# ScalarE's small jobs parted around the exponentials in the neighbourhood attention of a hybrid encoder layer

## The chip, the cores and the metric

The kernel runs on one core of a Trainium2 chip. The time is that of the whole execution on the device in microseconds (us); lower is better. Of the core's engines the text speaks of PE (TensorE, matmuls; PEld are its weight loads), ACT (ScalarE), DVE (VectorE), POOL (GpSimd, which also issues loads) and SP (SyncE, which issues transfers, among them the transposes that the DMA engines do). Each engine works through its own list of instructions in order and waits at an instruction for the results of others.

## The reference

One layer over 1024 tokens of width 1024. One projection of the normalised input gives the columns of two head groups; group A attends to all tokens, group B to a neighbourhood on the token grid of 16 rows by 64 columns. Both are gated, joined, projected, added to the input and normalised.

```python
proj = rmsnorm(x, norm_gain) @ w_in                      # 1024 x 3328
q_a, k_a, v_a, g_a, q_b, k_b, v_b, g_b = split(proj)     # 512, 128, 128, 512, 4 x 512
q_a, k_a = rope(rmsnorm(q_a)), rope(rmsnorm(k_a))
o_a = softmax(q_a k_a^T / 8) v_a                         # 8 query heads, 2 key heads, all 1024 keys
o_b = softmax(q_b k_b^T / 8 + bias, in the window) v_b   # 8 heads, window 8 rows x 16 columns
mixed = concat(o_a * silu(g_a), o_b * silu(g_b))
out = rmsnorm(x + mixed @ w_out, final_norm_gain)
```

Everything is float32; the kernel works with pairs of half-precision numbers, a high and a low half, so that each product is three matmuls (high by high, high by low, low by high).

## The kernel before

Tokens are handled as 8 row blocks `u` of 128, weights as groups `g` of 256 columns: 0 to 12 for the input projection (11 and 12 are the gates of group B), 13 to 16 for the output projection. A group is loaded by POOL (`load_w`, L207), squared by ACT for its scale (`squares`, L357, four quarters, accumulating into `wss`), and split into halves (`split`): each quarter's high half on ACT (`hi`, L399), its low half on DVE (`lo`, L404). When the last quarter is split, the load of group `g + 2` is let go; for groups 15 and 16 the freed buffer takes two rows of the input for the residual (`have_x2`).

The stages follow each other: normalising and transposing x, the projections, group A's attention (64 slots, `a_qk`), and group B's attention. Group B's stage has 32 slots, one for each row block (in the order `ORDER` = 0, 7, 1, 2, ... 6) and pair of heads. In slot `i`, counted from 0:

- PE computes the scores of pair `i` (`b_scores`, L810 and L813, into one of three PSUM banks `sb` a head), then a filling of projection matmuls (L489) for the gates or the output, and the products with the values of pair `i - 3` (`b_pv`, L860 to L862);
- DVE makes the low half of pair `i - 1` (`b_lo`, L840), SP transposes both halves (L842), then DVE adds the bias to the scores of pair `i` and takes the maximum (`b_qk`, L831, two instructions, `nm`), which frees the banks; the results `t` go round three buffers;
- ACT takes two exponentials (L833) and the high halves of both (L835).

Around this small jobs are handed to ACT and DVE by the class `Flow`: `job(eng, cost, fn, delay, late, key)` puts a piece of work on a list, and `step` writes one slot: `pre`, ACT's jobs, `first` (here `b_lo` and `b_qk`), `mid`, DVE's jobs, `post`, the filling of PE, `last` (here `b_pv`). `work(eng)` takes jobs in order of `late` (0 is urgent) and age; those that are not urgent are taken only while the slot's budget lasts, which is `base[0] + 0.654 n - base[1]` for ACT and `- base[2]` for DVE, with `n` chunks of filling. So all of ACT's jobs of a slot stand ahead of its exponentials, and DVE's behind its bias additions. The jobs are:

- quarters: squares (0.75 or 1.0), `hi` and `lo`;
- gates (`g_gen`): ACT's tanh (L689), then DVE's product with the gate (L694), in the same slot; when a gate's product with the tanh is there, group B's heads are divided by their sums (L869 to L872) and multiplied in by POOL (L874);
- finished rows (`os_start`): the sum of squares of the mixed row, half of it on ACT (`sq`, L897) and half on DVE (`scale`, L901), POOL's root (L904), then in the next slot two casts on ACT (`hi`, L909) and their low halves on DVE (`lo`, L913), which SP transposes (L922). `ms[0]` is group A's half of the row, `ms[1]` group B's, and the squares' junk goes into the row's own buffer `mhl`, of which two take turns behind the fourth row;
- final norms (`fin_a`, L995, and `fin_b`).

POOL also issues the residual's loads (`load_x2`, L960).

## Time and profile before

| | us |
|---|---|
| runs shown | 568.47, 569.99, 571.41 |
| median | 569.99 |
| the profiled execution | 570.9, span 569.1 |
| stage of group B (32 slots) | about 366 to 516 |
| DVE busy in it | 59.75 of 74 to 440, 61.45 of 76 behind |

A row of the timeline is start, duration, engine, line, operation, result `<-` operands, shape and count, and in brackets the idle time just before with what ended it. A group's row ends in busy time, mean nanoseconds of one, and idle time before it. A row of waits is engine and line, for whom, total, times and longest. A row of stretches gives busy time and count of each engine, then the granted clock of PE as a share, the DMA engines' share and GB/s.

### The profile page before, as it was taken

Reading aid. Unit: us, or ns where it says so; the run is one execution under the profiler, and the core shown is the slowest. Engines: PE = TensorE matmul, PEld = TensorE weight load, DVE = VectorE, ACT = ScalarE, POOL = GpSimd, SP = SyncE. Lnnn points to the kernel's source line nnn. Section 1 sums busy time; section 2 is a strip of 40 time slices with the busy share of each in tenths; the row PEclk is TensorE's granted clock in tenths of the full one; section 3 lists DMA queues with packets and bytes.
Section 4 is the critical chain, followed back from the end, with each engine's and each line's share of the span. In section 5 each row is a group of like instructions: output and inputs, shape, how many; then the busy total and the mean of one; then the engine's idle time right before and its main releaser. Section 6 shows DMA issues by size and latency. Waiting matters only on the chain.

```text
span 569.1 us, 13780 instructions
## 1 busy us (share of the span) xinstructions
PE 516.9 (91%) x5583; PEld 403.1 (71%) x5583; DVE 444.3 (78%) x911; ACT 368.7 (65%) x583; POOL 154.2 (27%) x181
## 2 busy tenths in 40 slices
PE   2567989989999999999999999997999888999994
PEld 0455877768887555578888888886777566778883
DVE  3689688989977978788789897578788886987632
ACT  5546466958869669686786868285876686663211
POOL 2394887670000000000000034433621221213100
PEclk9978899999999999999999999999899798999998
DMA  8999739789999999998999989336576999998712
GB/s 242 214 182 225 128 61 212 126 144 182 228 229 185 172 213 196 197 186 162 237 162 200 187 185 184 97 75 155 125 128 114 192 199 204 164 149 156 202 38 74
DMA packets 244513, 95.47 MB, mean 168 GB/s; under 512 B 235489, under 2 KB 236001, under 8 KB 242530
## 3 DMA queue, kind: packets, MB, share of 16 engines
q1 hardware_dynamic: 240850, 73.89, 71.2%
q0 software_dynamic: 3312, 19.92, 12.6%
q10 hardware_dynamic: 288, 0.79, 0.5%
q8 instruction: 43, 0.70, 0.5%
q14 instruction: 20, 0.16, 0.1%
HBM read 29.56 MB, written 4.19 MB: 59 GB/s over the span
## 4 chain that ended last, share of the span: by engine, by line
PE 51%; DVE 11%; ACT 5%; issue 5%; DMA 5%; POOL 1%; SPq 0%; DVEq 0%; POOLq 0%; ACTq 0%
PE pj L489 19%; PE kb L489 7%; PE pjb L489 5%; DMA ar<-ar 4%; PE s L720 4%; PE s L722 4%; PE sb L489 3%; DVE ar L831 3%; PE pv L753 3%; PE pv L754 3%; PE pv L752 3%; ACT rq L833 2%; DVE ar L840 2%; DVE whl L404 1%; ACT ar L835 1%
## 5 line engine op out<-in xcount | busy, mean ns | idle before, releaser
L489 PEld LDWEIGHTS <-hT 128*128 128x128 f16 x2112 | 206.1, 100 | 61.3 <-DMA hT<-ar 17.3
L489 PE MATMUL pj<-whl,hT 128*128 128x256 f16 x1680 | 201.2, 278 | 22.4 <-DMA hT<-ar 10.4
L729 ACT ACTIVATE ar<-s,nm,sm 128x1024 f32<-128x1024 f32 x64 | 76.9, 1202 | 55.0 <-DVE nm L727 54.5
L727 DVE CUSTOM_DVE_ANT_0 ar<-s,sm 128x1024 bf16<-128x1024 f32 x64 | 82.0, 1281 | 32.4 <-PE s L722 32.1
L489 PEld LDWEIGHTS <-ar 128*128 128x128 f16 x768 | 74.6, 99 | 11.2 <-issue 2.2
L735 DVE TENSOR_TENSOR ar<-ar 128x1024 f16<-128x1024 f32 x64 | 79.5, 1242 | 1.4 <-ACT ar L730 1.4
L730 ACT ACTIVATE ar<-ar 128x1024 f16<-128x1024 f32 x64 | 67.6, 1057 | 2.1 <-DVE sum L759 0.3
L833 ACT ACTIVATE rq<-ar,nm 128x384 f32<-128x384 f32 (+1 forms) x64 | 34.1, 579 | 33.4 <-DVE nm L831 32.8
L489 PE MATMUL pjb<-whl,ar 128*128 128x256 f16 x408 | 48.9, 278 | 0.0
L489 PE MATMUL kb<-hT,whl 128*128 128x512 f16 x192 | 44.5, 379 | 0.0
L840 DVE SCALAR_TENSOR_TENSOR ar<-rq,ar 128x768 f16<-128x768 f32 (+1 forms) x32 | 30.8, 962 | 15.8 <-ACT ar L835 15.5
L753 PE MATMUL pv<-va,ar 128*128 128x64 f16 x384 | 40.0, 194 | 0.0
L752 PE MATMUL pv<-va,ar 128*128 128x65 f16 x384 | 39.9, 193 | 0.0
L754 PE MATMUL pv<-va,ar 128*128 128x65 f16 x384 | 39.8, 192 | 0.0
L752 PEld LDWEIGHTS <-ar 128*128 128x128 f16 x384 | 35.5, 96 | 5.3
L404 DVE SCALAR_TENSOR_TENSOR whl<-raw,sm,whl 128x512 f16<-128x512 f32 x52 | 39.1, 790 | 0.0
L753 PEld LDWEIGHTS <-ar 128*128 128x128 f16 x384 | 35.3, 97 | 5.3
L720 PE MATMUL s<-kTa,rq 128*128 128x512 f16 x128 | 38.0, 379 | 0.0
L207 POOL DMA_DIRECT2D raw<-in_w_dram x11 | 6.7, 608 | 111.3 <-ACT ar L730 89.0
L489 PE MATMUL pjb<-whl,hT 128*128 128x256 f16 x288 | 35.5, 281 | 0.0
L754 PEld LDWEIGHTS <-ar 128*128 128x128 f16 x384 | 35.4, 99 | 0.0
L874 POOL TENSOR_TENSOR ar<-ar,qkg 128x256 f32<-128x256 f32 x16 | 17.5, 1091 | 65.6 <-DVE qkg L872 64.4
(173 smaller groups left out, 972.7 us busy)
## 6 DMA issues: line engine op xcount, KB each, us to landing
raw<-in_w_dram POOLq DMA_DIRECT2D x11, 1024.0 KB, 7.4
raw<-in_wo_dram POOLq DMA_DIRECT2D x4, 1024.0 KB, 5.4
ar<-in_x_dram SPq DMA_DIRECT2D x7, 512.0 KB, 6.6
khh<-ar SPq DMA_DIRECT2D x16, 128.0 KB, 3.3
x2b<-in_x_dram POOLq DMA_DIRECT2D x4, 512.0 KB, 5.8
x<-in_x_dram POOLq DMA_DIRECT2D x4, 512.0 KB, 6.8
out_dram<-x2b SPq DMA_DIRECT2D x8, 256.0 KB, 3.6
out_dram<-x SPq DMA_DIRECT2D x7, 256.0 KB, 2.9
```

The costliest lines, as they stand in the source:

```text
L404: dve.scalar_tensor_tensor(wp[g][1][:, q], raw[g][:, q], col(S_ + g), wp[g][0][:, q], op0=OP.mult, op1=OP.subtract)
L489: pe.matmul(*o[0], **o[1])
L720: pe.matmul(s[:, c * 512:(c + 1) * 512], q, kTa[:, 4 * c:4 * c + 4, hh], start=True, stop=False)
L727: dve.tensor_tensor_reduce(out=hl[:, 1].bitcast(BF16), in0=s, in1=col(SHA).to_broadcast([P, 1024]), scale=col(NSA), scalar=3e38, op0=OP.ad ...
L729: act.activation(p32, s, AF.Exp, bias=nm, scale=col(SCA))
L730: at(0, "mid", lambda: act.activation(hl[:, 0], p32, AF.Copy))
L735: dve.tensor_tensor(hl[:, 1], p32, hl[:, 0], op=OP.subtract)
L752: pe.matmul(o, pt[:, kt], va[:, kt, hh, v_hi], start=kt == 0, stop=False)
L753: pe.matmul(o[:, :D], pt[:, kt], va[:, kt, hh, v_lo], start=False, stop=False)
L754: pe.matmul(o, pt[:, 8 + kt], va[:, kt, hh, v_hi], start=False, stop=kt == 7)
L833: act.activation(p32[:, e], t[:, e], AF.Exp, bias=nm, scale=-1.0)
L840: dve.scalar_tensor_tensor(hl[:, 1], p32, 2.0 ** 14, hl[:, 0], op0=OP.mult, op1=OP.subtract)
```

## The change

`step` now passes a limit, `early` = 1.2, to ACT's jobs ahead of `first`; after `first` (with its exponentials) ACT's list is taken up again with what is left of the budget. The limit is looked at before each job. It holds in group B's stage alone. In that stage DVE's budget is smaller by 0.5 and ACT's by 0.3, and a quarter's low half counts 1.0 instead of 0.72. The two squares of a finished row are exchanged between ACT and DVE, and their junk goes to spare strips of the tiles `rest` (for the first row DVE's still to its own buffer).

```diff
-BASE_A, BASE_B = (1.8, 2.6, 2.9), (1.7, 1.3, 1.5)
+BASE_A, BASE_B = (1.8, 2.6, 2.9), (1.7, 1.6, 2.0)
...
-    def work(self, eng):
+    def work(self, eng, early=None, more=False):
         b = self.budget.get(eng)
-        self.left[eng] = 1e9 if b is None else min(self.left.get(eng, 0.0), 0.5 * b) + b
+        if not more:
+            self.left[eng] = 1e9 if b is None else min(self.left.get(eng, 0.0), 0.5 * b) + b
+        stop = -1e9 if early is None else self.left[eng] - early
         while True:
             due = sorted(j for j in self.jobs if j[3] == eng and j[1] <= self.slot and (j[0] == 0 or j[4] / 2 < self.left[eng]))
-            if not due:
+            if not due or self.left[eng] <= stop:
                 return
...
-        self.work("act")
+        self.work("act", self.early)
         if first:
             first()
+        if self.early is not None:
+            self.work("act", more=True)
...
-            job("dve", 0.72, lo, i, delay=0, late=0.5 if g > 11 else 2, key=g)
+            job("dve", 1.0 if "b" in late else 0.72, lo, i, delay=0, late=0.5 if g > 11 else 2, key=g)
...
         def sq():
-            act.activation(osp[u][0][:, cs[1]].bitcast(BF16), ms[1], AF.Square, accum_out=t[:, 0:1])
+            act.activation(late["r"][0][:, 2048:2560].bitcast(BF16), ms[0], AF.Square, accum_out=t[:, 0:1])
             job("dve", 0.95, scale, delay=0, late=0, key=("os", u))

         def scale():
-            dve.tensor_tensor_reduce(out=osp[u][0][:, cs[0]].bitcast(BF16), in0=ms[0], in1=ms[0], scale=1.0, scalar=t[:, 0:1],
+            junk = late["r"][1][:, 2048:2560] if k else osp[u][0][:, cs[1]]
+            dve.tensor_tensor_reduce(out=junk.bitcast(BF16), in0=ms[1], in1=ms[1], scale=1.0, scalar=t[:, 0:1],
...
-    fl.base = BASE_B
+    fl.base, fl.early = BASE_B, 1.2
```

Lines of the changed kernel are 5 to 6 higher than those of the kernel before (L404 is L409 there, L694 is L699). PE's list keeps its order but for the sums of squares of groups 14 to 16 (L373, four matmuls of one column each), which move by one to three slots. Three places show what moves.

DVE in slots 5 to 7 (`nm7_4` to `nm1_0`; `rest` are the halves of group 13). Before:

```order
L694 SCALAR_TENSOR_TENSOR ar_78<-ar_78,pjb1_5197 128x2x256
L404 SCALAR_TENSOR_TENSOR rest1_5102<-raw13_5039,sm_97,rest0_5101 128x512 x4
L421 RECIPROCAL sm_97<-sm_97 128x1
L840 SCALAR_TENSOR_TENSOR ar_78<-rq_79,ar_78 128x512
L831 ISA ar_78,nm7_6_5507<-sb2_5113,rq_79,sm_97 128x256
```

Now:

```order
L699 SCALAR_TENSOR_TENSOR ar_78<-ar_78,pjb1_5197 128x2x256
L409 SCALAR_TENSOR_TENSOR rest1_5102<-raw13_5039,sm_97,rest0_5101 128x512
L845 SCALAR_TENSOR_TENSOR ar_78<-rq_79,ar_78 128x512
L836 ISA ar_78,nm7_6_5497<-sb2_5113,rq_79,sm_97 128x256
L836 ISA nm7_6_5497 128x1
L836 ISA ar_78,nm7_7_5500<-sb0_5111,rq_79,sm_97 128x256
L836 ISA nm7_7_5500 128x1
L874 RECIPROCAL sumb0_0_5504<-pvb0_5115 128x4
L875 TENSOR_TENSOR sumb0_0_5504<-sumb0_0_5504,sm_97 128x4
L877 TENSOR_TENSOR qkg_85<-pvb0_5115,sumb0_0_5504 128x256
L409 SCALAR_TENSOR_TENSOR rest1_5102<-raw13_5039,sm_97,rest0_5101 128x512
```

The four low halves stood in one slot and now stand one a slot; the other two follow in the next two slots.

ACT in slots 15 and 16 (`nm2_6` to `nm3_1`; `mhl`, `os`: the finished rows 7 and 1; `pjb0`: a gate's bank; `whl14`, `raw15`: weights). Before:

```order
L909 ACTIVATE mhl7_5891<-ar_78,os7_5890 128x512 x2
L689 ACTIVATE ar_78<-pjb0_5196,sm_97 128x512
L833 ACTIVATE rq_79<-ar_78,nm2_6_6016 128x384
L833 ACTIVATE rq_79<-ar_78,nm2_7_6019 128x384
L835 ACTIVATE ar_78<-rq_79 128x768
L897 ACTIVATE mhl1_6035,os1_6034<-ar_78 128x512
L399 ACTIVATE whl14_6036<-raw14_5372,sm_97 128x512 x4
L833 ACTIVATE rq_79<-ar_78,nm3_0_6090 128x384
```

Now:

```order
L362 ACTIVATE rest0_5101,wss15_0_5670<-raw15_5668 128x512
L362 ACTIVATE rest0_5101,wss15_1_5671<-raw15_5668 128x512
L362 ACTIVATE rest0_5101,wss15_2_5672<-raw15_5668 128x512
L915 ACTIVATE mhl7_5887<-ar_78,os7_5886 128x512 x2
L838 ACTIVATE rq_79<-ar_78,nm2_6_6008 128x384
L838 ACTIVATE rq_79<-ar_78,nm2_7_6011 128x384
L840 ACTIVATE ar_78<-rq_79 128x768
L694 ACTIVATE ar_78<-pjb0_5196,sm_97 128x512
L902 ACTIVATE rest0_5101,os1_6027<-ar_78 128x512
L404 ACTIVATE whl14_6029<-raw14_5427,sm_97 128x512 x2
L838 ACTIVATE rq_79<-ar_78,nm3_0_6081 128x384
```

The tanh of the gate moved behind the exponentials and the cast of slot 15, squares moved ahead of the row's casts, the row's square writes to `rest0`, and two of the four quarters moved behind the exponentials of slot 16. Slot 17 has the same form: its tanh stands behind its exponentials. DVE's product with the gate keeps its place directly behind the bias additions of slots 15 and 17.

POOL around the last weight load (`raw16`) and the first loads of the residual. Before:

```order
L207 DMA raw16_6147<-in_wo_dram 128x2048
L874 TENSOR_TENSOR ar_78<-ar_78,qkg_85 128x256
L960 DMA x2b_6277<-in_x_dram 128x1x1024
L874 TENSOR_TENSOR ar_78<-ar_78,qkg_85 128x256
L960 DMA x2b_6277<-in_x_dram 128x1x1024
```

Now:

```order
L879 TENSOR_TENSOR ar_78<-ar_78,qkg_85 128x256
L381 TENSOR_TENSOR sm_97<-wss15_0_5670,mh_83 128x1
L966 DMA x2b_6271<-in_x_dram 128x1x1024
L212 DMA raw16_6273<-in_wo_dram 128x2048
L879 TENSOR_TENSOR ar_78<-ar_78,qkg_85 128x256
L966 DMA x2b_6271<-in_x_dram 128x1x1024
```

The weight load moved behind the first `x2b`, which waits on POOL for the last projection from `hT`. The first load into group 15's freed buffer, likewise, moved behind one more product (L874).

## The prediction

> **What bounds the kernel now.** I read the page first, then sums over stretches, then the waits of PE, and last the timeline around each of them. The page's first line, and three stretches: the stage that the change touches up to its middle, the rest of it, and the output projections behind it.

> ```profile
> span 569.1 us, 13780 instructions
> ...
> core 0: us, PE busy (x) PEld busy (x) DVE busy (x) ACT busy (x) POOL busy (x), PEclk, DMA share, GB/s
> 366.00:440.00 74.00, 69.66 (x759) 55.73 (x760) 59.75 (x151) 52.62 (x103) 27.54 (x29) 0.98 0.59 118
> 440.00:516.00 76.00, 65.76 (x718) 50.91 (x717) 61.45 (x165) 51.21 (x94) 16.99 (x21) 0.93 1.02 179
> 516.00:561.50 45.50, 45.45 (x443) 40.61 (x440) 24.97 (x71) 9.77 (x25) 7.12 (x12) 1.00 0.45 120
> ```

> The 32 slots of the neighbourhood stage lie between 366 and 516. Behind 516 PE has no gap (45.45 of 45.50), so whatever PE gains before 516 arrives whole at the end. Before 366 no engine's order changes. What PE loses in the stage is idle time and half clock. The waits of PE from 366 to 516, four of the nine gaps in its timeline (in brackets the idle time and what ended it), and the three stretches at half clock:

> ```profile
> PE sb L810 <- DVE nm L831: 7.0, 5, 3.3
> PE pvb L860 <- DMA ar<-ar: 4.0, 2, 2.7
> PE pvb L860 <- DVE qkg L872: 3.4, 2, 2.3
> ...
> 396.71 0.19 PE L860 MATMUL pvb<-rq,ar 128*128 128x65 f16 x1 [2.28 <-DVE qkg L872]
> 422.92 0.19 PE L860 MATMUL pvb<-ar 128*128 128x65 f16 x1 [1.15 <-DVE qkg L872]
> 443.37 0.48 PE L810 MATMUL sb<-khh,qTb 128*128 128x384 f16 x1 [3.35 <-DVE nm L831]
> 468.28 0.32 PE L810 MATMUL sb<-khh,qTb 128*128 128x384 f16 x1 [1.45 <-DVE nm L831]
> 478.90 0.20 PE L860 MATMUL pvb<-rq,ar 128*128 128x65 f16 x1 [2.68 <-DMA ar<-ar]
> ...
> 398.00:401.40 3.40, 3.40 (x19) 2.44 (x17) 2.41 (x7) 2.65 (x6) 3.40 (x4) 0.51 1.10 309
> 442.40:449.20 6.80, 5.83 (x27) 3.69 (x27) 6.53 (x17) 3.62 (x7) 1.15 (x1) 0.50 1.04 227
> 480.00:483.40 3.40, 3.40 (x17) 2.26 (x16) 2.74 (x10) 3.37 (x6) 0.55 (x1) 0.50 0.83 228
> ```

> The idle time is 7.0 + 4.0 + 3.4 = 14.4 us: by the scores 0.91, 3.35, 0.39, 1.45 and 0.90, by transposes 2.68 and 1.30, by DVE's division 2.28 and 1.15. The gaps of 2.28, 3.35 and 2.68 us each have a half-clock stretch beginning during them or within 1.5 us of their end; the gaps up to 1.45 have none. So I price a gap above 2 us with its clock: half of the PE time at half clock, 1.7 + 2.9 + 1.7 = 6.3 us. At stake are 20.7 us in all.

> Without them PE needs (74 - 4.3 - 1.7) / 18 = 3.8 us a slot. DVE is close behind: 61.45 us over the last 14 slots are 4.4 us a slot. PE may be one slot ahead of DVE, since scores go round three banks, two a slot. A slot in which DVE (or ACT, for which DVE waits at L840) needs more than about 7.6 us therefore stops PE, and one of 4 us does not.

> **The change part by part.**

> *(a) Quarters spread, slots 4 to 13: -6.0 us.* The two gaps at 387.69 (0.91) and 396.71 (2.28) stand behind bunches of four low halves on DVE:

> ```profile
> 381.91 3.76 DVE L404 SCALAR_TENSOR_TENSOR whl<-raw,sm,whl 128x512 f16<-128x512 f32 x4
> ...
> 391.71 2.73 DVE L404 SCALAR_TENSOR_TENSOR rest<-raw,sm,rest 128x512 f16<-128x512 f32 x4
> ```

> With the new costs the first bunch is three and one, the second one a slot. The slot of the first gap is shorter by one low half (0.9) and the five small factor operations behind it (0.9), the slot of the second by three low halves (2.0), and 0.8 to 1.8 us earlier already. Both gaps should go, and with the second its half clock (1.7). What moved out lands in slots 7 to 10, where DVE itself waited for ACT or PE, so it costs nothing there; without that cover it would be 0.7 us a quarter. At 422.92 (1.15) the chain came through an ACT that ran three squares and two casts ahead of the exponentials; now the squares fill time in which the casts waited. 0.91 + 2.28 + 1.70 + 1.15 = 6.0; if the last gap and the clock stay, 3.2.

> *(b) Squares exchanged, slot 16: -6.3 us.* ACT's square of the gated row waited for a transpose of the row before, because its junk output went into the buffer being transposed:

> ```profile
> 436.73 0.63 ACT L897 ACTIVATE mhl<-ar 128x512 bf16<-128x512 f32 x1 [4.58 <-DMA ar<-mhl]
> ...
> 437.35 2.54 ACT L399 ACTIVATE whl<-raw,sm 128x512 f16<-128x512 f32 x4
> 439.80 1.11 ACT L833 ACTIVATE rq<-ar,nm 128x384 f32<-128x384 f32 x2
> ...
> ACT mhl L897 <- POOL ar L874: 5.5, 4, 1.6
> ```

> Behind it stood four quarters and then the exponentials, for which DVE and then PE waited (the 3.35 us gap). Now the junk goes to a spare strip, the row squared is group A's, finished long before, and only two quarters stay ahead. That takes 4.58 + 1.27 us out of ACT's path, more than the gap. With the 2.9 of clock: 6.3, and 3.35 if the clock is lost anyway. The other waits of ACT for POOL at this square (5.5 us in four) end too; DVE's square now needs POOL's product, but it stands a whole slot behind it, so I cost it at nothing. Uncovered it would be POOL's 1.1 us once a row.

> *(c) Jobs behind the exponentials, slots 15 and 17: +9.1 us.* The new limit of 1.2 us is spent by the two casts of a mixed row (2 x 0.72 in the table of costs). The tanh of a gate is then put behind the exponentials of the same slot, but DVE's product that needs it still stands directly behind that slot's bias additions. Today tanh comes first:

> ```profile
> 428.35 1.34 ACT L909 ACTIVATE mhl<-ar,os 128x512 f16<-128x512 f32 x2 [0.57 <-POOL os L904]
> 429.60 0.67 ACT L689 ACTIVATE ar<-pjb,sm 128x512 f32<-128x512 f32 x1
> 430.17 1.11 ACT L833 ACTIVATE rq<-ar,nm 128x384 f32<-128x384 f32 x2
> ...
> 430.29 0.69 DVE L694 SCALAR_TENSOR_TENSOR ar<-ar,pjb 128x512 f32<-128x512 f32 x1 [0.25 <-ACT ar L689]
> ...
> 431.72 1.88 DVE L913 SCALAR_TENSOR_TENSOR mhl<-ar,os,mhl 128x512 f16<-128x512 f32 x2
> ...
> 433.59 0.94 DVE L840 SCALAR_TENSOR_TENSOR ar<-rq,ar 128x768 f16<-128x768 f32 x1
> ...
> L357 ACT ACTIVATE rest<-raw 128x512 bf16<-128x512 f32 x16 | 10.0, 624 | 0.3
> L835 ACT ACTIVATE ar<-rq 128x768 f16<-128x768 f32 (+1 forms) x32 | 25.3, 790 | 1.0
> L840 DVE SCALAR_TENSOR_TENSOR ar<-rq,ar 128x768 f16<-128x768 f32 (+1 forms) x32 | 30.8, 962 | 15.8 <-ACT ar L835 15.5
> ```

> In slot 15 ACT will do, after the cast of slot 14, three squares (3 x 0.62, with their sums some 2.3 us), two casts (1.3), two exponentials (1.1), the cast (0.8) and tanh (0.6): 6.1 us. DVE in that time has L840 (0.9) and two bias additions (1.2), so it waits some 4 us, and behind it stand the product (0.7), the division of the finished heads (0.8), both L913 (1.9) and the next L840 (0.9). Slot 17 is alike: two quarters, a square, two casts, the exponentials, the cast and tanh are 6.0 us against some 3 of DVE's, a wait of about 3. From the additions of slot 15 to those of slot 18 DVE then needs about 22 us, where PE has work for four slots, 15, and comes with less than a microsecond in hand: I take two gaps of PE, 2.6 and 3.1 us. Both are above 2 us, so with half clock of 3.4 us each it is 5.7 + 3.4 = 9.1. Bounds: 3 if DVE's lead hides half of it and the clock holds, 12.5 if each behaves like the gap of 3.35 with 6.8 us at half clock.

> *(d) Slots 20 to 23: -1.8 us.* Group 15's four quarters (ACT 2.5, DVE 2.7 us) stood in one slot with a row's square; spread, they end the gaps of 0.39 and 1.45. Bound: 0.

> *(e) Transfers: -2.7 us.* The burst before 478.9, as POOL issues it and as its transfers land (last column: us to landing), beside an undisturbed transpose and one with a single load (rows of three short stretches):

> ```profile
> 441.39 0.62 POOL L207 DMA_DIRECT2D raw<-in_wo_dram  x1 [1.88 <-DVE sm L421]
> ...
> 449.76 0.58 POOL L960 DMA_DIRECT2D x2b<-in_x_dram  x1 [3.24 <-PE sb L489]
> ...
> x2b<-in_x_dram POOLq DMA_DIRECT2D x1, 512.0 KB, 6.7
> x<-in_x_dram POOLq DMA_DIRECT2D x1, 512.0 KB, 7.9
> ar<-mhl SPq DMA_TRANSPOSE x2, 7.6
> ar<-ar SPq DMA_TRANSPOSE x1, 10.4
> ...
> ar<-ar SPq DMA_TRANSPOSE x1, 3.6
> ...
> ar<-ar SPq DMA_TRANSPOSE x1, 6.3
> ...
> 478.88 0.62 DVE L831 CUSTOM_DVE_ANT_0 ar<-sb,ar,sm 128x384 f32<-128x384 f32 x1 [3.88 <-DMA ar<-ar]
> ```

> Alone a transpose lands after 3.6 us, with one load beside it after 6.3, with two loads and two row transposes after 10.4. Group 15 is finished two slots later, so the first residual load `x` leaves this burst: about 3 of the 3.88 us go. PE's share was 2.68 + 1.7 = 4.4; I take 2.7. Against it, the last weight load (1 MB) is issued two slots later too, behind the first `x2b` on POOL, so transposes of slots 18 to 20 meet both. They have two slots until they are needed, 8 us, against an estimated 7 to 9. Bounds 0 and -4.4.

> *(f) Nothing:* the gaps of 0.90 (506.66) and 1.30 (514.44, a transpose beside a load) are not touched, or are replaced where group 16's quarters now fall. No instruction is added; operation counts and sizes stay.

> Sum: -6.0 - 6.3 + 9.1 - 1.8 - 2.7 = -7.7 us against the profiled execution's own 570.9 (its span of 569.1 and 1.8 around it): **563.2 us**. The median of the runs, 569.99, lies 0.9 lower, inside their spread, so I leave it there.

> [...]

> **The rivals.**

> *Slower: a job behind the exponentials stops DVE wherever its other half is due in the same slot.* Besides the two tanh this holds for quarters in slots 4, 20 and 26 (the third or second quarter's low half needs an ACT instruction behind the cast). Price: 12.5 for the tanh, 3 x 1.3 for the quarters (an exponential and a cast less what DVE does meanwhile), and (d) and (e) come to nothing: -6.0 - 6.3 + 12.5 + 3.9 = +4.1, **575.0**. It decides once DVE's waits for ACT at L694 and L404 exceed about 14 us. For it: DVE already waits 15.5 us for ACT at L840. Against: PE's slot of lead. 12 in 100.

> *No change: transfers bound the second half.* From 440 to 516 the DMA engines are busy at a share of 1.02 and the bytes stay. If transposes then land when they land now, any lead reaching slot 18 is given back: **570**. Against: shares of 1.04 to 1.10 stand in shorter stretches above. 18 in 100.

> *All of it: DVE hides the tanh.* 14.4 + 6.3 gone: **550**. Against: DVE at 4.4 us a slot. 8 in 100.

> [...] 10 in 100.

> **How the numbers follow.** The forecast has 52 in 100, its own range 558 to 567. A measurement here tells about 0.5% from no change, so faster is below 567.1 and slower above 572.8. Faster: the forecast but for its edge, the case of 550 and most of the last, 0.65. Same: no change and those edges, 0.20. Slower: its rival and what no-change spills over, 0.15. The range takes in no change and reaches to 556, halfway to the case of 550, (c) small and (e) whole: 556 to 571.

> **What would show it.** (a) no gap of PE between 385 and 425 above 0.6 us and full clock there; (b) no wait of ACT's square; (c) DVE waiting 3 to 4 us for ACT ahead of the gate's product in two places about 13 us apart, each followed by a gap of PE at the scores; (e) no transpose above 9 us. I am wrong if the two tanh waits are absent, or larger than 5 us each, or if waits for transposes grow beyond today's 4.0 us of PE.

## The result, and the profile after

Over twenty runs of each kernel the change takes 568.58 us against 571.66 (medians), a ratio of 0.9946 with a 95% interval from 0.9921 to 0.9972: faster by 3.1 us, where 7.7 had been forecast. The execution that was profiled took 566.36 us (span 564.5), 4.5 less than the one profiled before; it lies 2.2 below its own median, the earlier one 0.8 below its own. So the two traces show a difference of 4.5 us, some 1.5 more than the medians. The ratios, here and below, leave out an execution that is over 1.5% longer than the fastest of its kernel, and two of the traces below are of such executions, that of sq_only (582.02 us) and that of vf_scalar (575.49 us), each the longest of its kernel's runs.

The same three stretches of the kernel after the change; the stage now ends 4.5 us earlier, so the bounds are shifted by that:

```profile
span 564.5 us, 13778 instructions
...
366.00:440.00 74.00, 69.22 (x740) 55.10 (x738) 62.05 (x154) 55.00 (x108) 28.34 (x28) 0.98 0.61 121
440.00:511.50 71.50, 63.89 (x743) 50.68 (x742) 60.39 (x162) 49.61 (x94) 18.46 (x23) 0.98 1.02 190
511.50:557.00 45.50, 45.41 (x442) 40.56 (x440) 25.43 (x71) 8.49 (x22) 6.92 (x10) 1.00 0.44 120
```

The part behind the stage is unchanged: 45.41 of 45.50 us busy. All of the gain was made in the 32 slots. What PE waited for there, five of its gaps, and the waits of DVE that changed most:

```profile
PE sb L815 <- DVE nm L836: 9.1, 6, 2.7
PE pvb L865 <- DVE qkg L877: 1.5, 2, 0.8
PE pvb L865 <- DMA ar<-ar: 1.4, 1, 1.4
...
391.77 0.27 PE L815 MATMUL sb<-khh,qTb 128*128 128x256 f16 x1 [0.97 <-DVE nm L836]
395.71 0.19 PE L865 MATMUL pvb<-rq,ar 128*128 128x65 f16 x1 [0.73 <-DVE qkg L877]
435.31 0.32 PE L815 MATMUL sb<-khh,qTb 128*128 128x384 f16 x1 [2.33 <-DVE nm L836]
447.71 0.32 PE L815 MATMUL sb<-khh,qTb 128*128 128x384 f16 x1 [2.74 <-DVE nm L836]
466.31 0.32 PE L815 MATMUL sb<-khh,qTb 128*128 128x384 f16 x1 [1.88 <-DVE nm L836]
...
DVE ar L845 <- ACT ar L840: 7.5, 11, 1.5
DVE ar L699 <- ACT ar L694: 6.6, 2, 3.6
...
DVE ar L836 <- DMA ar<-ar: 0.5, 1, 0.5
```

The waits for transposes fell from 4.0 us to 1.4 and those for the division from 3.4 to 1.5, but the waits at the scores rose from 7.0 to 9.1. Two of those are new, 2.33 and 2.74 us, 12.4 us apart. Ahead of each of the two, DVE stands still for a tanh:

```profile
430.50 0.69 DVE L699 SCALAR_TENSOR_TENSOR ar<-ar,pjb 128x512 f32<-128x512 f32 x1 [3.62 <-ACT ar L694]
...
442.91 0.69 DVE L699 SCALAR_TENSOR_TENSOR ar<-ar,pjb 128x512 f32<-128x512 f32 x1 [2.97 <-ACT ar L694]
```

These are the two waits that term (c) describes. Where the 4.5 us came from is best seen in the time from DVE's first running maximum of slot 0 to those of later slots, read from the timeline; executions reach slot 0 up to 12 us apart, and this leaves that out. All runs that are told of below stand in one table:

| kernel (label of the run) | slots 0 to 15 | 15 to 19 | 19 to 24 | 24 to the end |
|---|---|---|---|---|
| before | 62.36 | 22.64 | 27.36 | 90.21 |
| after | 58.70 | 24.95 | 23.87 | 90.01 |
| sq_only | 62.09 | 20.89 | 31.54 | 89.69 |
| no_limit | 60.29 | 18.19 | 29.15 | 89.19 |
| tanh_free | 58.08 | 18.20 | 28.63 | 90.04 |
| vf_scalar | 58.52 | 24.95 | 28.64 | 89.95 |
| after_loads | 58.72 | 24.95 | 24.64 | 93.08 |
| tf_loads | 58.06 | 18.20 | 30.98 | 93.56 |
| narrow_dve | 59.37 | 24.94 | 24.35 | 89.97 |
| tf_loads_nd | 59.12 | 18.20 | 28.30 | 93.59 |
| tf_sp | 58.07 | 18.20 | 26.64 | 88.43 |
| tf_sp_raw | 58.08 | 18.19 | 25.85 | 88.89 |
| after_sp_raw | 58.71 | 24.95 | 23.59 | 88.87 |
| before_sp_raw | 61.75 | 22.62 | 24.66 | 90.47 |
| sq_sp_raw | 61.72 | 19.84 | 24.58 | 90.25 |
| nl_sp_raw | 60.31 | 18.18 | 26.01 | 87.89 |
| tf_sp_raw_nd | 58.58 | 18.19 | 26.59 | 88.83 |

Before and after differ by -3.7, +2.3, -3.5 and -0.2 us, in all -5.0; slot 0 is reached 0.5 later. The forecast had -6.0 for (a), +2.8 for (b) and (c), -4.5 for (d) and (e), and 0.

### The profile page after: what moved, and what is told of

Its sections match the earlier page's. It is cut to its first block, busy times and chain, and to the rows that moved or that the text cites. A ratio compares the mean times of both kernels' runs of the same rounds, so it can differ in the third digit from the quotient of the medians.

```text
span 564.5 us, 13778 instructions
## 1 busy us (share of the span) xinstructions
PE 515.5 (91%) x5583; PEld 402.4 (71%) x5583; DVE 446.0 (79%) x911; ACT 367.8 (65%) x583; POOL 157.2 (28%) x181
## 4 chain that ended last, share of the span: by engine, by line
PE 51%; DVE 9%; ACT 8%; issue 5%; DMA 4%; SPq 0%; POOL 0%; DVEq 0%; POOLq 0%; ACTq 0%
PE pj L494 19%; PE kb L494 7%; PE pjb L494 5%; PE s L725 4%; PE s L727 4%; ACT rq L838 3%; PE sb L494 3%; PE pv L758 3%; DMA ar<-ar 3%; PE pv L759 3%; PE pv L757 3%; ACT ar L840 3%; DVE ar L836 2%; DVE ar L845 2%; DMA x2b<-in_x_dram 1%
## 5 line engine op out<-in xcount | busy, mean ns | idle before, releaser
L494 PEld LDWEIGHTS <-hT 128*128 128x128 f16 x2112 | 204.9, 100 | 58.8 <-issue 16.2
L494 PE MATMUL pj<-whl,hT 128*128 128x256 f16 x1680 | 201.6, 278 | 20.9 <-DMA hT<-ar 7.8
L494 PEld LDWEIGHTS <-ar 128*128 128x128 f16 x768 | 74.6, 99 | 11.7 <-issue 2.6
L494 PE MATMUL pjb<-whl,ar 128*128 128x256 f16 x408 | 47.4, 273 | 0.0
L494 PE MATMUL kb<-hT,whl 128*128 128x512 f16 x192 | 44.5, 379 | 0.0
L409 DVE SCALAR_TENSOR_TENSOR whl<-raw,sm,whl 128x512 f16<-128x512 f32 x52 | 38.7, 770 | 2.8 <-ACT whl L404 2.8
L845 DVE SCALAR_TENSOR_TENSOR ar<-rq,ar 128x768 f16<-128x768 f32 (+1 forms) x32 | 30.7, 959 | 7.9 <-ACT ar L840 7.5
L404 ACT ACTIVATE whl<-raw,sm 128x512 f16<-128x512 f32 x52 | 34.0, 709 | 1.4 <-POOL sm L381 1.4
## 6 DMA issues: line engine op xcount, KB each, us to landing
ar<-in_x_dram SPq DMA_DIRECT2D x7, 512.0 KB, 6.3
x2b<-in_x_dram POOLq DMA_DIRECT2D x4, 512.0 KB, 6.9
x<-in_x_dram POOLq DMA_DIRECT2D x4, 512.0 KB, 6.2
```

Source lines behind the costliest of these rows:

```text
L409: dve.scalar_tensor_tensor(wp[g][1][:, q], raw[g][:, q], col(S_ + g), wp[g][0][:, q], op0=OP.mult, op1=OP.subtract)
L494: pe.matmul(*o[0], **o[1])
L845: dve.scalar_tensor_tensor(hl[:, 1], p32, 2.0 ** 14, hl[:, 0], op0=OP.mult, op1=OP.subtract)
```

## The experiments

Times are ratios to the kernel before on the same chip, with their 95% interval. In the kernels that move the tanh, lines behind the edit are one higher than in the changed kernel.

### One part of the change at a time

**sq_only**: the kernel before with the squares exchanged, and nothing else of the change.

```diff
-            act.activation(osp[u][0][:, cs[1]].bitcast(BF16), ms[1], AF.Square, accum_out=t[:, 0:1])
+            act.activation(late["r"][0][:, 2048:2560].bitcast(BF16), ms[0], AF.Square, accum_out=t[:, 0:1])
...
+            junk = late["r"][1][:, 2048:2560] if k else osp[u][0][:, cs[1]]
...
```

> The kernel before with nothing but the exchange of the two squares and their new junk strips. My theory: ACT's 4.58 us wait for the row transpose goes, with it PE's gap of 3.35 us at the scores of slot 16 and its half clock (2.9 us): about -6.3 us, ratio 0.989, and no wait of a square for a transpose. Rival, transfers bound the second half: the lead is handed back at the transposes of slots 20 to 31; PE's waits for transposes grow from 4.0 us to over 7 and the ratio is 0.995 to 1.000.

Measured: 0.9959 (0.9915 to 1.0002). The gap of 3.35 us at slot 16 is replaced by two small ones, and a gap at a transpose appears three slots later:

```profile
449.88 0.32 PE L810 MATMUL sb<-khh,qTb 128*128 128x384 f16 x1 [0.64 <-DVE nm L831]
455.02 0.32 PE L810 MATMUL sb<-khh,qTb 128*128 128x384 f16 x1 [1.12 <-DVE nm L831]
468.13 0.23 PE L860 MATMUL pvb<-rq,ar 128*128 128x65 f16 x1 [5.14 <-DMA ar<-ar]
```

Slots 15 to 19 are 1.75 us shorter, slots 19 to 24 are 4.2 longer. The ratio lies in the rival's range, and in this trace its mechanism is seen: what the squares give is taken by transposes. The trace is of the longest of the seven runs, 9.5 us late already at slot 0, so it doesn't tell how much of this the others had.

**no_limit** and **tanh_free**: the changed kernel with the two waits for a tanh taken away in two ways. The first drops the limit; the second lets the tanh go ahead of its slot's other jobs and leaves it out of the limit.

```diff
 no_limit
-    fl.base, fl.early = BASE_B, 1.2
+    fl.base, fl.early = BASE_B, None
 tanh_free
-    job("act", 0.7, lambda: act.activation(th, pt, AF.Tanh, ...), late=0)
+    job("act", 0.7, lambda: act.activation(th, pt, AF.Tanh, ...), late=-1 if "b" in late else 0)
...
 in work():
             self.left[eng] -= j[4]
+            stop -= j[4] if j[0] < 0 else 0
```

> The changed kernel without the limit of 1.2 us: all of a slot's small jobs of ACT stand ahead of the exponentials again. My theory: DVE's two waits for a tanh (3.62 and 2.97 us) go, and with them PE's gaps of 2.33 and 2.74 us and the half clock between them (1.7 us): -6.8 us against the changed kernel, 0.983 of the one before. Rival, the limit earns elsewhere what it costs here: quarters and squares ahead of the exponentials make DVE wait longer for the casts of the exponentials, new gaps of PE in slots 10 to 22, and the ratio stays at 0.993 to 0.997.

> The changed kernel, but a tanh goes ahead of the other jobs of its slot and does not count against the limit, so it and up to two casts stand ahead of the exponentials; quarters and squares stay behind. My theory: as without the limit, the two waits and their gaps go, -6.8 us against the changed kernel: 0.983 of the one before. Rival, DVE's own work (4.4 us a slot) bounds slots 15 to 18: the waits go but PE waits for DVE in the same slots and at most 3 us are won: 0.989 to 0.995.

Measured: 0.9928 (0.9895 to 0.9960) and 0.9915 (0.9885 to 0.9945). Both take DVE's two waits and PE's two gaps away, and both shorten slots 15 to 19 by the same 6.8 us (24.95 to 18.2). That is the price of (c). But neither time falls by that, and both traces have one long gap at a transpose (6.20 and 5.36 us). Nine of tanh_free's ten runs lie from 561.46 to 568.22 us; the one that was profiled is the shortest. The trace of tanh_free, the gap and the transfers from 438 to 462:

```profile
455.13 0.24 PE L866 MATMUL pvb<-ar 128*128 128x65 f16 x1 [5.36 <-DMA ar<-ar]
...
q1 hardware_dynamic: 7987, 2.00, 65.5%
q0 software_dynamic: 576, 2.62, 46.0%
...
x2b<-in_x_dram POOLq DMA_DIRECT2D x4, 512.0 KB, 8.5
raw<-in_wo_dram POOLq DMA_DIRECT2D x1, 1024.0 KB, 7.6
ar<-ar SPq DMA_TRANSPOSE x4, 13.9
```

Transposes that land after 3.7 us alone take 13.9 here, beside three residual rows and the last weight group. In the changed kernel the same loads stand at the same places, and the transposes landed within 8.3 us. Its row for 447 to 471:

```profile
q0 software_dynamic: 720, 3.15, 49.8%
...
ar<-ar SPq DMA_TRANSPOSE x6, 7.2
```

It isn't that the tanh only hid a wait of the same length. Counted from the issue of the first residual row, the weight load goes out after 2.37 us in both kernels, the next transpose after 3.10 and the second row after 6.29; that transpose landed after 7.6 us in one kernel and 13.9 in the other, and PE asked for it here 8.6 us after its issue. Of the four traces without the waits for a tanh and with these loads on POOL, all have a gap of 5.4 to 7.3 us at this place (no_limit, tanh_free, tf_loads, tf_loads_nd); of the four with these waits (after, after_loads, narrow_dve, vf_scalar) one has long transposes there, vf_scalar with 12.9 and 15.6 us, and its gaps are 2.67 and 1.10. What makes a transpose long in one execution and not in the other was not found.

**vf_scalar**: what kept the gaps of 0.97 and 0.73 us at 391 and 395? In slot 6 of the changed kernel a product of two columns took fifteen times its length (2.40 us against 0.16 in the trace before), until two additions on POOL had ended:

```profile
388.11 2.40 DVE L487 TENSOR_TENSOR vf<-sm 128x1 f32<-128x1 f32 x1
...
388.53 1.96 POOL L786 TENSOR_TENSOR ar<-ar,rest 128x384 f32<-128x384 f32 x2
```

```diff
-        dve.tensor_tensor(t, col(RC + VB + hh), col(G2 + GB - GATE + hh), op=OP.mult)
+        dve.tensor_scalar(t, col(RC + VB + hh), col(G2 + GB - GATE + hh), None, op0=OP.mult)
```

> The changed kernel with one instruction of another form: the 128x1 product of two columns, which took 2.40 us in the changed kernel's trace and 0.16 us in the one before, is a multiplication by a per-partition scalar, so that it reads one tensor. My theory: with two tensors from SBUF it was held up by the two POOL products that ran from 388.53 to 390.49; in the new form it takes under 0.3 us, PE's gap of 0.97 us at the scores behind it and that of 0.73 behind the next slot's division go: -1.7 us against the changed kernel, ratio 0.991 to 0.992. Rival, it waited for something else (its operand): it still takes over 2 us and the ratio is 0.994 to 0.996. Second rival: it is short now, but the next instruction of DVE takes the time.

Measured: 0.9944 (0.9914 to 0.9975). The second rival holds: the product is short, and the next instruction takes the time, again until POOL's pair ends (393.17 + 1.96 = 395.13):

```profile
392.75 0.21 DVE L487 TENSOR_SCALAR vf<-sm 128x1 f32<-128x1 f32 x1
393.00 2.16 DVE L488 TENSOR_SCALAR sm<-vf 128x4 f32<-128x4 f32 x1
...
393.17 1.96 POOL L786 TENSOR_TENSOR ar<-ar,rest 128x384 f32<-128x384 f32 x2
```

In no_limit a third instruction meets the pair (390.03 to 391.99), the addition at L845: it starts at 389.64 and takes 2.90 us, where the one of the slot before takes 0.68. So it is not this one form. Three different instructions, one of them with a single tensor as its operand, started 0.42, 0.17 and 0.39 us ahead of the pair and ended 0.02, 0.03 and 0.55 us behind its end. That is all the rows show; what holds the instruction up was not shown.

### The transfers: how many bytes, or beside what

**after_loads**, **tf_loads**: 2.5 MB of loads are held back, in the changed kernel and in tanh_free. The third residual row thus goes out in slot 21 in place of 20, the fourth in slot 25 in place of 21. In tf_loads the edits of tanh_free come on top.

```diff
-X2_BEHIND = {0: (0, 1), 1: (2,), 2: (3,), 3: (4,), 4: (5,), 5: (6,), 6: (7,)}
+X2_BEHIND = {0: (0, 1), 3: (2,), 4: (3,), 5: (4, 5), 6: (6, 7)}
...
-        if i == 25:
+        if i == 29:
             late["gout"] = one.tile([P, 1024], F32, tag="gain", name="gain_o")
```

> The changed kernel with 2.5 MB of loads held back: the third and fourth residual row come behind the row transposes of the fourth and fifth mixed row, the rows of the output's second half behind the sixth and seventh, the gain of the output norm four slots later; nothing else. My theory now: two waits lie one behind the other in slots 15 to 20, first DVE's for the two tanh, then PE's for transposes that meet the loads (4.9 us in the run with the tanh moved); the changed kernel pays only the first, so taking load away wins at most its gap of 1.42 at the transpose near 510: ratio 0.992 to 0.995. Rival, the transfers cost the changed kernel as much in most executions, only not in the one profiled: 0.985 to 0.989.

> The tanh ahead of its slot and outside the limit, and the 2.5 MB of loads held back. My theory: with both waits gone the gap of 5.36 us at slot 20 goes (transposes of slots 18 to 20 land within 9 us in place of 13.9 and 15.3), and the ratio is 0.980 to 0.984. Rival, transposes alone fill the DMA engines (about 0.74 of their time from 440 to 516): they still land after 10 us or more and the ratio stays at 0.989 to 0.993.

Measured: 0.9983 (0.9948 to 1.0017) and 0.9968 (0.9944 to 0.9993): worse than without the edit, outside what either theory gave. The gaps at transposes of tf_loads:

```profile
459.37 0.24 PE L866 MATMUL pvb<-ar 128*128 128x65 f16 x1 [7.29 <-DMA ar<-ar]
...
511.54 0.20 PE L866 MATMUL pvb<-rq,ar 128*128 128x65 f16 x1 [3.30 <-DMA ar<-ar]
```

The first is longer with 0.5 MB less beside it, the second (3.08 in after_loads) stands where the loads were moved to. My theory that the amount of data makes the wait falls. The trace's packet records tell more: in tf_loads the small packets of a transpose last 18 ns when it runs alone. From 455 to 459 us the mean is 117, because 220 of 563 packets last 50 to 708 ns, while 4 KB packets of a residual row from POOL's queue trickle in between (180 KB); the engines move 45 to 104 GB/s through most of it, against some 290 a little later, when transposes run alone. But a load of POOL's queue beside a transpose is not enough: in the changed kernel's trace 893 KB of such loads were moved from 455 to 459, and none of the 1537 transpose packets beside them lasted over 26 ns. So the question for the next runs is whether the long packets go when the loads leave POOL's queue.

**tf_sp**, **tf_sp_raw**, **after_sp_raw**: so the loads go through SP's queue, in line with the transposes, with the same issue points: in tanh_free the residual rows, then the last weight group too, then both in the changed kernel.

```diff
-            pool.dma_start(x2[u], rows_of(x, u, 1024, 0, 1024))
+            sp.dma_start(x2[u], rows_of(x, u, 1024, 0, 1024))
 and in tf_sp_raw and after_sp_raw
-        pool.dma_start(raw[g], w[g] if g < 13 else wo[g - 13])
+        (pool if g < 16 else sp).dma_start(raw[g], w[g] if g < 13 else wo[g - 13])
```

> The tanh ahead and outside the limit; the residual rows are loaded through SP's queue, in line with the transposes, in place of POOL's (the last weight group stays with POOL). My theory: a transpose is held up because a load from the other queue is moved at the same time (its packets took 18 ns alone and 50 to 150 ns beside such a load); in one queue they follow one another, transposes of slots 18 to 20 land within 10 us in place of 14 to 16, PE's gap of 5.4 to 7.3 us at slot 20 shrinks below 2, ratio 0.980 to 0.985. Rival, the bytes alone make it: the transposes wait behind the loads instead, the gap stays at 3 us or more and the ratio at 0.989 to 0.994.

> As the last, with the last weight group's 1 MB through SP's queue too. My theory: no load is left in the other queue in slots 18 to 21, transposes land within 10 us and the gap is below 2 us: 0.979 to 0.984. Rival: the transpose behind the weight group waits for its 1 MB as well, a gap of 3 us or more: 0.989 to 0.994.

> The changed kernel, the tanh where the change put them, with residual rows and the last weight group through SP's queue. My theory: the two waits for a tanh still take their 6 us, so that transposes have slack; only the gap of 1.42 us near 510 and the chance of a longer one go: 0.990 to 0.995. Rival, transfers cost the changed kernel most of what the forecast missed: 0.984 to 0.989.

Measured: 0.9817 (0.9781 to 0.9854), 0.9810 (0.9773 to 0.9848) and 0.9921 (0.9890 to 0.9953). All three ratios are as this theory had them. In the trace of tf_sp, which keeps one load on POOL's queue, the slowest transpose still took 10.5 us and the gap 2.09, just over what the theory allowed. The five runs of tf_sp_raw lie between 558.35 and 560.81 us, closer together than those of tanh_free. Its trace over the same 24 us, and the gaps above 1 us:

```profile
453.33 0.20 PE L866 MATMUL pvb<-ar 128*128 128x65 f16 x1 [1.10 <-DMA ar<-ar]
460.31 0.33 PE L816 MATMUL sb<-khh,qTb 128*128 128x384 f16 x1 [2.19 <-DVE nm L837]
...
q1 hardware_dynamic: 10724, 5.16, 100.7%
...
x2b<-in_x_dram SPq DMA_DIRECT2D x4, 512.0 KB, 7.5
raw<-in_wo_dram SPq DMA_DIRECT2D x1, 1024.0 KB, 6.7
ar<-ar SPq DMA_TRANSPOSE x5, 7.8
```

5.16 MB went through this queue where tanh_free moved 4.62 through both, and transposes landed after 7.8 us in place of 13.9. In the six traces with all these loads in SP's queue no transpose from slot 15 on took over 9.5 us. The loads changed three things at once, the queue, the engine that issues them and the kind of queue that the page names (`hardware_dynamic` for `software_dynamic`); which of them counts was not separated. With the tanh left where the change put them (after_sp_raw) 6 to 7 us are missing again: 24.95 against 18.19 in slots 15 to 19.

### The terms again, with the transposes out of the way

**before_sp_raw** (the kernel before, loads in SP's queue), **sq_sp_raw** (the same with the squares exchanged), **nl_sp_raw** (no_limit with loads in SP's queue): edits as above.

> The kernel before with nothing but residual rows and the last weight group loaded through SP's queue. My theory: only its waits for transposes go (gaps of 2.68 and 1.30 us and the half clock behind the first, 1.7 us): 0.990 to 0.994; the gap of 3.35 at slot 16 stays, since no load is near it. Rival: loads in line with transposes delay those as much as they delayed them from the side, 0.997 to 1.002.

> The same with the squares exchanged too. My theory: the term forecast for the squares (3.35 us of gap and 2.9 us of half clock) now arrives whole: 0.011 below the run with the loads alone, that is 0.979 to 0.984. Rival, the lead is taken back further on by DVE, as the transposes took it when the squares were exchanged alone: at most 0.005 below.

> The changed kernel without the limit of 1.2 us, loads in SP's queue. My theory: the limit wins nothing that the costs and the exchange don't, so this equals the run with the tanh ahead of the limit and the loads in SP's queue, 0.979 to 0.984. Rival: squares and quarters ahead of the exponentials cost 2 us or more in slots 10 to 22, 0.985 to 0.990.

Measured: 0.9941 (0.9915 to 0.9967), 0.9898 (0.9862 to 0.9935), 0.9805 (0.9767 to 0.9843). The first is as expected, at the upper edge. The exchange of the squares brings 0.0043, not 0.011; here the rival's bound holds, though the two intervals overlap. In the traces, the gap at slot 16 of before_sp_raw and then those of sq_sp_raw in its place:

```profile
440.90 0.32 PE L810 MATMUL sb<-khh,qTb 128*128 128x384 f16 x1 [3.33 <-DVE nm L831]
```

```profile
441.47 0.32 PE L810 MATMUL sb<-khh,qTb 128*128 128x384 f16 x1 [0.62 <-DVE nm L831]
446.61 0.32 PE L810 MATMUL sb<-khh,qTb 128*128 128x384 f16 x1 [1.12 <-DVE nm L831]
```

Slots 15 to 19 go from 22.62 to 19.84: the term is worth 2.8 us. The limit, whose effect nl_sp_raw shows against tf_sp_raw, can't be told from nothing in the ratios (0.9805 and 0.9810); in the single traces slots 0 to 15 are 2.2 us shorter with it and slots 24 to the end 1.0 longer. Against the kernel before both are faster by 11 us, against the changed one by some 8.

**narrow_dve**, **tf_loads_nd**, **tf_sp_raw_nd**: the eight additions of POOL's, of which a pair holds up DVE in slot 6, are given to DVE itself, in the changed kernel, in tf_loads and in tf_sp_raw.

```diff
-        pool.tensor_tensor(bias[hh][:, h4i], bias[hh][:, h4i], late["inner"], op=OP.add)
+        dve.tensor_tensor(bias[hh][:, h4i], bias[hh][:, h4i], late["inner"], op=OP.add)
```

> The changed kernel with the eight additions 128x384 that POOL makes in slots 6 to 9 made by DVE at the same places. My theory: the 2.2 us by which an instruction of DVE is held in slot 6 until POOL's pair ends are gone, against two additions of some 0.5 us on DVE; the gap of 0.97 us at slot 6 and that of 0.73 at slot 7 go: the stage is shorter by 1 to 1.7 us, ratio 0.991 to 0.993. Rival, DVE's own 4 us more take back what the collision cost: 0.994 to 0.997, and gaps in slots 7 to 9.

> All three: tanh ahead and outside the limit, loads held back, the additions on DVE. My theory: the terms add, 0.978 to 0.982. Rival: with DVE as the bound the last of them wins nothing, 0.983 or more.

> The tanh ahead, all these loads in SP's queue, and the eight additions of slots 6 to 9 on DVE in place of POOL. My theory: 1 to 1.7 us less than with the additions on POOL, 0.978 to 0.979. Rival: DVE's own work takes it back in slots 7 to 12, 0.981 to 0.983.

Measured: 0.9932 (0.9897 to 0.9968), 0.9994 (0.9957 to 1.0031), 0.9842 (0.9800 to 0.9884). Gaps of narrow_dve up to the first tanh:

```profile
390.96 0.19 PE L865 MATMUL pvb<-rq,ar 128*128 128x65 f16 x1 [0.44 <-DVE qkg L877]
399.76 0.19 PE L865 MATMUL pvb<-ar 128*128 128x65 f16 x1 [0.61 <-DVE qkg L877]
408.21 0.19 PE L865 MATMUL pvb<-rq,ar 128*128 128x65 f16 x1 [0.92 <-DVE qkg L877]
417.20 0.19 PE L865 MATMUL pvb<-ar 128*128 128x65 f16 x1 [0.99 <-DVE qkg L877]
432.65 0.32 PE L815 MATMUL sb<-khh,qTb 128*128 128x384 f16 x1 [2.32 <-DVE nm L836]
```

This execution reaches slot 0 3.3 us before that of the changed kernel. The product of 2.40 us takes 0.16 here, the gap of 0.97 has gone and that of 0.73 is 0.44, as the theory of the held-up DVE says. Two others, of 0.61 and 0.92, have come and the one of 0.75 is 0.99, as the rival says: slots 0 to 15 take 59.37 us against 58.70. With the loads in SP's queue the ratio is 0.9842 against 0.9810. So DVE pays for the additions either way. The collision is shown; that it can be had cheaper is not.

## Why the prediction was right or wrong

The direction was right: 3.1 us faster, where 7.7 had been forecast; the traces differ by 5.0 from slot 0 on. The sum is made of PE's idle time and of PE's time at half clock, so it can be set beside PE's own account, from slot 0 to the end. A matmul at half clock counts as busy for longer (in the trace after, those of 128x256 at L494 last 404 ns on average from 436.2 to 439.5, at half clock, and 272 to 273 from 440 to 463), so the clock is found in the busy time. (How much of (e)'s 2.7 us is clock the sum leaves open: 1.7 if all of the clock goes, 1.1 if the 2.68 of gap and the 1.7 of clock shrink alike.)

| | before | after | difference | forecast |
|---|---|---|---|---|
| PE idle | 22.22 | 20.02 | -2.2 | -4.8 to -5.4 |
| PE busy | 180.35 | 177.51 | -2.8 | -2.3 to -2.9 |

**The step that failed** is that gaps of PE were put at nothing: in (a) "Both gaps should go", and the third gap with them, and in (d) "they end the gaps of 0.39 and 1.45". 2.46 us stayed in (a) and 2.16 in (d), 4.6 us in all for which the sum has no term. Terms (c) and (e) cost less idle time than forecast and give some 2 us back. In all these places DVE is late, and taking one piece of its work out of a slot moved the wait to the next piece.

The total of **"I price a gap above 2 us with its clock"** came right, but by luck. In the stage the half clock fell from 13.7 to 6.8 us, as the sum has it; but it was to come behind both waits for a tanh, and it came behind one of them (2.33 us), not behind the longer (2.74), and once behind the gap of 1.88 of (d), where none was forecast. Nor is this clock a term that can be added to a gap, as three comparisons show. First, the kernel before spent 6.8 us at half clock behind its gap at slot 16 and before_sp_raw 3.4; slots 15 to 19 take 22.64 and 22.62 us. Second, the changed kernel has half clock between its two waits for a tanh and gaps of 2.33 and 2.74; vf_scalar and narrow_dve have none between them and gaps of 2.33 and 4.13, and of 2.32 and 4.14; the four slots take 24.95, 24.95 and 24.94. after_loads has 7.1 us of half clock in these slots where the changed kernel has 3.4, and takes 24.95 too. Where DVE is the one that is late, PE at half clock arrives later at a wait that it would have had anyway. Third, the stretch in (a) is missing in before_sp_raw, whose gaps up to slot 15 are 0.9 longer in its place; it is 0.6 us faster up to there, not 1.7. By these comparisons most of the table's -2.8 is no gain beside the idle time: with full clock in both kernels it would have gone into waits for DVE. No run has that.

Term by term, by the slots of the table further up:

- *(a) -6.0, measured -3.7.* Full clock, and three gaps smaller but not gone: 0.97, 0.73 and 0.75 stayed of 0.91, 2.28 and 1.15. By moving the last quarter a slot on, the change set five small instructions of DVE beside POOL's pair of additions, and one of them took 2.40 us. Before, the same product took 0.16, while POOL was issuing a load. The prediction looked for DVE's own work in the slot and not for its neighbour on POOL; in narrow_dve, without that neighbour, DVE's own work makes other gaps. The gap of 0.75 isn't in tanh_free; its cause was not followed. Of the 3.7 us the limit brings 1.6: no_limit takes 60.29 for these slots.
- *(b) -6.3, measured -2.8 by itself* (sq_sp_raw against before_sp_raw). No square of ACT waits for a transpose any more, as forecast. 1.7 of the 3.35 us of gap come back as two smaller waits for DVE; the rest of the 2.8 is PE's busy time, 1.2 where the clock had been priced at 2.9.
- *(c) +9.1, measured +6.8.* Two waits of 3.62 and 2.97 us, 12.4 us apart, each followed by a gap at the scores: 2.6 and 3.1 forecast, 2.33 and 2.74 seen. The clock fell once and not twice. (b) and (c) together were +2.8 and came to +2.3; that the net was right hides two errors that cancel.
- *(d) -1.8, measured +0.3.* The gaps of 0.39 and 1.45 became 0.28 and 1.88. Two residual additions, a division and the two low halves of a mixed row (1.88 us) still stand between DVE's maxima of slots 21 and 22, as before, and between the two additions DVE now waits 0.41 us for a residual row.
- *(e) -2.7; (d) and (e) together -4.5, measured -3.5.* The gap of 2.68 has gone and DVE's wait of 3.88 fell to 0.5; no transpose of this execution whose landing the trace has took over 8.3 us.

The rival "transfers bound the second half" (18 in 100) is not what the changed kernel does, which is faster, but in sq_only's trace it is what happens, and without the waits for a tanh it is the next limit. Whether it also makes the difference between the 5.0 us of the two traces and the 3.1 of the medians is open. vf_scalar, which has the changed kernel's order of instructions but for one form, met transposes of 12.9 and 15.6 us and took 28.64 us for slots 19 to 24 in place of 23.87; but that execution was the longest of its ten, and how often the changed kernel meets this was not counted. The last 10 in 100, counted mostly to faster, were on a case without new stretches at half clock; the trace after has two, behind gaps of 2.33 and 1.88 us.

## What to carry to other kernels

When a wait is removed, ask which one stands next in line at the same place, and try the two separately and together: the exchange of the squares and the tanh moved ahead each brought little alone; the change, the tanh ahead and the loads in SP's queue brought eleven microseconds together. Before a gap is put at nothing, add up what else the late engine has to do in that slot, and look at what runs on its neighbour (here two additions on POOL, beside which 0.16 us became 2.40). A stretch at half clock cost nothing to be seen where DVE was the late one (22.64 and 22.62 us for four slots with 6.8 and 3.4 us of it), so add it to a gap only if somebody waits for PE behind it. If an ACT job is put behind other work, its other half on DVE has to move with it, or DVE stands still in between (3.62 and 2.97 us here).

## What the runs showed of the hardware

```profile
442.90:446.30 3.40, 2.07 (x32) 1.72 (x30) 3.32 (x8) 0.00 (x0) 1.16 (x1) 1.00 0.01 3
446.30:449.70 3.40, 1.99 (x17) 1.41 (x17) 3.30 (x9) 1.91 (x4) 1.10 (x2) 1.00 0.98 169
463.40:466.80 3.40, 1.52 (x26) 0.88 (x23) 3.40 (x10) 0.44 (x1) 1.30 (x2) 1.00 1.13 225
466.80:470.20 3.40, 3.40 (x18) 2.39 (x17) 2.55 (x6) 3.14 (x8) 0.00 (x0) 0.51 1.15 237
```

In after_sp_raw none followed a step with 1.79 us of idle time and one followed a step with 1.85. Behind a step at half clock another one followed at 0.62 us of idle time in it (no_limit) and at 0.93 (before), and none at 0.54 (after_loads). So it hung on where they fell that each of the three gaps above 2 us had half clock in the kernel before: tf_sp has gaps of 2.09 and 2.21 and no half clock in the whole stage.

**Beside loads of POOL's queue a transpose on SP's queue took three to four times as long in some of these traces, and not in others.** It took 3.6 to 3.7 us alone (before, issued at 407.88, 425.15 and 435.29), and beside these loads 11 to 16.2 in slots 19 and 20 of no_limit, tanh_free, tf_loads, tf_loads_nd and vf_scalar, but 7.6 to 9.4 in after, after_loads and narrow_dve; with the same loads in SP's own queue it took at most 9.5. Why some packets of a transpose last 50 to 708 ns in one trace (tf_loads), and none over 26 beside more load in another (after), stays open.
